# A four-layer hybrid trunk on one core: raw-x projections in the first mixer and paired score products in the attention

## The chip, the core and the metric

The kernel runs on one core of one Trainium2 chip, in one launch. Its metric is the device time in microseconds; less is better. An execution is a straight program: each engine works through its own list of instructions in order and waits on semaphores for the others. TensorE is called PE here, its weight loads PEld, VectorE is DVE, ScalarE is ACT, GpSimd is POOL, and SP issues most DMAs.

## What is computed

A trunk on x of 512 tokens by 1024 features, in float32: a gated DeltaNet mixer, a SwiGLU feed-forward, a dilated attention, and a second feed-forward. Each of the four normalises its input first and adds its output to x. The parts that the change touches:

```python
def _rmsnorm(x, w):
    y = x * lax.rsqrt(jnp.mean(x * x, axis=-1, keepdims=True) + RMS_EPS)
    return y * w
...
    proj = h @ w_in                      # h = _rmsnorm(x, w): q, k, v, gate z, and a, b
    qkv = jax.nn.silu(_causal_depthwise_conv(proj[..., :n_qkv], conv_w))
...
    o = o * norm_w * jax.nn.silu(z)      # o: the chunked delta rule, normalised
...
    scores = jnp.einsum("brnqhd,brnkhd->brnhqk", qb, kb) * (dh ** -0.5)
    logits = jnp.where(valid[:, None], scores + bias, -jnp.inf)
    p = jnp.exp(logits - m)              # m: the row maximum
```

The mixer has 8 heads of 128 features each for q, k, v and z. The attention has 24 heads of 64 features in three groups of 8: group 0 looks at the 128 last positions, groups 1 and 2 at every 4th and every 16th position further back. The factor of the norm, one number per token, can be taken out of a projection: (x * r) @ W = (x @ W) * r.

## The kernel before

Activations lie as features by tokens: a *page* is an SBUF tile of 128 features by 512 tokens, a *bank* one of PE's 8 accumulators of 128 by 512 float32. A projection is a *job* (`gemm_steps`, the matmul at L455): a weight tile, streamed in from HBM as `wraw`, is split into a high and a low half (`wh` by ACT, `wl` by DVE or POOL), the input likewise, and for each of 8 slices of the input three matmuls go into one bank: high·high, high·low, low·high. So a job is 24 matmuls of 512 columns.

The order of the work is set at build time by a planner, `Weave`. It runs generators against a simulated clock for each engine, and what they issue as they are resumed is the program's order. `W.run` runs a job on PE; between two of its matmuls all generators that have become ready get their turn, so other products stand between projection matmuls. `Banks` are counters that share the 8 banks out: `main` (`mm`) for jobs, `sm` for short products, `chain` (`ch`) for chains that hold one long. In the first mixer these are 2, 3 and 3 (`BANKS`), in the attention 3, 2 and 3 (`ABANKS`). The order of the jobs stands in `JOBS` (first mixer) and `DJOBS` (attention).

**First mixer** (`start` L302, `gdn` L505). When x has arrived, `highs` and `lows` (L393 and L404) make high and low halves of x times the norm's weight, the *raw* halves, which the first three key jobs use (`RAW_KEYS`). Meanwhile squares of x are summed and `rb`, the factor of the norm spread over 128 partitions, is worked out. Then `normalised` (L412) multiplies the eight pages of x by `rb`, five on POOL (`NORM`) and three on DVE, and `highs` and `lows` run a second time on these. The other 29 jobs use the second halves. A q, k or v job (`conv_job` L619) is followed by its `post`: ACT reads the bank with the last of four convolution taps, DVE adds the other three (for two key heads two, POOL the third), then comes SiLU through a tanh. The bank is given back only behind the last tap. In the three raw jobs DVE first multiplies the bank by `rb` into a page and gives it back at once:

```python
                    if raw:
                        yield "rb", 0
                        V.tensor_mul(dst, ps, self.rb)
                        main.release(V)
```

A finished key head is turned to tokens by PE (`turn`, L442) and multiplied with itself (`mat`, L437). `solve` (L734) inverts the triangular systems in 32-wide blocks on POOL and DVE, `merge` (L774) joins them on PE, and `head` (L872) runs the heads. The gate job (`gate_job` L978) reads its bank once on ACT (tanh) and once on DVE.

**Attention** (`dilated` L1085). Two heads share a page: head 0 in partitions 0 to 63, head 1 in 64 to 127; there are four such pairs for each group. `near(p, h)` (L1329) makes the scores of one head in group 0, in two bursts of products (`mat`, L437) into one bank each: blocks 0 and 1 (128 and 256 columns), then 2 and 3 (256 and 256). `far(p, h)` (L1375) makes those of groups 1 and 2, four products of 128 columns to a burst. Each burst is followed by DVE's addition of the distances and by row maxima, after which the bank is free. The weights of the distance (`near_rest`, `far_rest`), the values (`value` L1417) and the output (`project_job` L1478) follow. Three lanes (`DLANES`) of `near` and `far` run side by side: head 0's near, head 1's near, and far of both heads in turn. The output projection's first job holds three tiles and takes pairs 0 to 2 for all of them (27 matmuls) before pair 3.

Every DVE, ACT and POOL operation is recorded on one helper's line, L85 (L83 in the changed kernel, where L455, L442 and L437 become L441, L428 and L423).

Of the kernel before, what the change touches and what calls it, by code (L numbers as in the profile page):

```python
# [11 lines left out]
F32 = mybir.dt.float32  # L12
F32R = mybir.dt.float32r
I32 = mybir.dt.int32
AF = mybir.ActivationFunctionType
# [4 lines left out]
T = 512  # L20
# [3 lines left out]
H = 8  # L24
# [9 lines left out]
AHEAD = True  # L34
# [4 lines left out]
DLANES = ('n0', 'n1', 'f0 f1')  # L39
# [20 lines left out]
NORM = (1, 2, 4, 6, 7)  # L60
# [3 lines left out]
ABANKS = {'mm': 3, 'sm': 2, 'ch': 3}  # L64
# [110 lines left out]
class Trunk:  # L175
# [126 lines left out]
    def start(self):  # L302
# [90 lines left out]
        def highs(n):  # L393
            for k in range(KD):
                yield "ready", n, k
                if n == "raw":
                    yield max(RAW + PACE * k - W.now, 0.0)
# [28 lines left out]
        on_pool = NORM  # L426
        W.spawn(normalised(self.G, on_pool))
        W.spawn(normalised(self.V, [k for k in range(KD) if k not in on_pool]))  # L428
# [76 lines left out]
    def gdn(self):  # L505
# [4 lines left out]
        with tc.tile_pool(name="gk", bufs=1) as gk, tc.tile_pool(name="gw", bufs=2) as gw:  # L510
            self.start()
            events, raw_events = ([("x", n, k) for k in range(KD)] for n in (0, "raw"))
            tiles, raws = ([lambda n=n, k=k: self.xs[n, k] for k in range(KD)] for n in (0, "raw"))
# [105 lines left out]
            def conv_job(ft, dst, acc, then):  # L619

                yield main
                raw = ft < 2 * H and ft - H in RAW_KEYS
                if raw:
                    yield "weights", 0
                w = next(self.ws)
                ps = self.bank()
                yield from self.gemm_steps(ps, w, raws if raw else tiles, raw_events if raw else events)

                def post():
                    nonlocal ps  # L630
                    if raw:
# [19 lines left out]
                    if not raw:  # L651
                        main.release(0.0)
# [325 lines left out]
            def gate_job(h):  # L978
# [106 lines left out]
    def dilated(self):  # L1085
# [11 lines left out]
        with tc.tile_pool(name="ak", bufs=1) as ak, tc.tile_pool(name="aw", bufs=2) as aw:  # L1097
            dist, slopes, bones, wqk, eps, place, block = self.dc
            fac = lambda i: rr[:, i].rearrange("p (g c) -> p g c", g=3)[:, :, :, None].to_broadcast([128, 3, NCH, 2])
# [21 lines left out]
            pages, scores, spaces = Banks(W, APAGES), Banks(W, SCORES), Banks(W, VALUES)  # L1121
# [207 lines left out]
            def near(p, h):  # L1329

                f = slice(h * 64, (h + 1) * 64)
                yield "k", 0, p
                yield "rq", p
                ts = []
                mx = aw.tile([128, NCH], F32, name="mx0", bufs=8)
                for bs in ((0, 1), (2, 3)):
                    yield scores
                    yield sm
                    ps = self.bank()
                    t = aw.tile([128, T], F32, name="pp", bufs=SCORES)  # L1340
                    o = 0
                    spans = []
                    for b in bs:
                        k0 = max(b - 1, 0)
                        n = (b + 1 - k0) * 128
                        mat(ps[:, o:o + n], qT[0, p][f, ch(b)], kT[0, p][f, k0 * 128:(b + 1) * 128])
                        spans.append((b, o, n))
                        o += n
                    for b, o, n in spans:
                        V.scalar_tensor_tensor(t[:, o:o + n], dist[0][:, 256 - n:], sd[p][:, 0, b, h:h + 1],  # L1350
                                               ps[:, o:o + n], op0=OP.mult, op1=OP.add)
                        yield V.next()
                        V.reduce_max(mx[:, b:b + 1], t[:, o:o + n], axis=AX)
                        yield V.next()
                    sm.release(V)
                    ts.append((t, spans))
# [337 lines left out]
```

## Time and profile before

| | |
|---|---|
| median of 3 runs | 1410.41 us (1409.83 to 1410.54) |
| the profiled execution | 1408.56 us |
| its span | 1406.7 us |
| instructions | 18298 |
| busy: PE, PEld | 1370.3 us, 1128.7 us |
| busy: DVE, ACT, POOL | 810.4 us, 598.0 us, 275.3 us |

The profiled execution is one of its own, and its span is the time from the first to the last recorded instruction. The first mixer ends at about 350 us; the attention takes the stretch from about 715 to 1030 us, with most of its scores and values between 860 and 1011. Rows of the trace below name a line, an engine, an operation, the tiles written and read (`page<-bank,cp` reads a bank and a column of constants and writes a page) and their shapes.

### The profile page before, as it was taken

To read this page: it belongs to the slowest core of one execution; us is meant where nothing else is said; L and a number is where in the kernel's file an instruction comes from. 1 tells how busy PE (TensorE), PEld (TensorE's weight loads), DVE (VectorE), ACT (ScalarE), POOL (GpSimd) and SP (SyncE) were. 2 spreads that over 40 slices of the span, in tenths; PEclk is the share of its full clock that TensorE was granted. 3 is DMA by queue.
4 is the path that set the end of the run, shared out by engine and by line. 5 is a ranking of instruction groups with operands and counts; after the bars stand their busy time and mean duration, and the time that the engine had idled before them with its cause. 6 is when DMAs were issued, how large, how long until landed. Compare 5 with 4: busy or idle time off the path is not lost.

```text
span 1406.7 us, 18298 instructions
## 1 busy us (share of the span) xinstructions
PE 1370.3 (97%) x7040; PEld 1128.7 (80%) x7040; DVE 810.4 (58%) x1458; ACT 598.0 (43%) x1276; POOL 275.3 (20%) x239
## 2 busy tenths in 40 slices
PE   8799989999999999999999999999989999999998
PEld 5578878878888888888888878789968888888887
DVE  7987655767555455534446456887576554554222
ACT  4665465863333333322246445565533333332221
POOL 6543800124111111112112111100051111110000
PEclk9999999999999999999999999999999999999999
DMA  4124240134232323333332222111013323233331
GB/s 160 57 64 120 75 122 31 31 121 124 82 105 90 105 90 102 88 96 97 97 87 93 90 75 76 45 31 61 31 60 105 105 90 105 90 102 100 109 110 60
DMA packets 48328, 122.52 MB, mean 87 GB/s; under 512 B 16624, under 2 KB 17008, under 8 KB 48240
## 3 DMA queue, kind: packets, MB, share of 16 engines
q1 hardware_dynamic: 47952, 121.21, 28.3%
q8 instruction: 55, 0.90, 0.3%
q14 instruction: 33, 0.27, 0.1%
q10 hardware_dynamic: 288, 0.14, 0.0%
HBM read 117.66 MB, written 3.67 MB: 86 GB/s over the span
## 4 chain that ended last, share of the span: by engine, by line
PE 83%; DVE 8%; ACT 3%; POOL 3%; issue 2%; DMA 1%; SPq 0%; DVEq 0%; ACTq 0%; POOLq 0%
PE bank L455 69%; PE bank L437 8%; DVE page L85 5%; PE bank L1201 3%; PE bank L442 2%; POOL xblk L85 2%; POOL tblk L85 1%; ACT page L85 1%; DVE wl L85 1%; ACT wh L85 0%; DMA wraw<-in_w 0%; ACT pp L85 0%; DVE ro L85 0%; PE bank L1265 0%; DVE rsqrt L85 0%
## 5 line engine op out<-in xcount | busy, mean ns | idle before, releaser
L455 PE MATMUL bank<-page,wh 128*128 128x512 f32 x2912 | 947.5, 394 | 11.4 <-DVE page L85 8.5
L455 PEld LDWEIGHTS bank<-page,wh 128*128 128x128 f32 x2912 | 546.3, 189 | 128.6 <-DVE page L85 11.0
L455 PE MATMUL bank<-page,wl 128*128 128x512 f32 x1632 | 642.4, 394 | 3.4 <-DVE wl L85 2.9
L85 ACT ACTIVATE wh<-wraw 128x512 fp32r<-128x512 f32 (+1 forms) x432 | 255.8, 616 | 468.3 <-PE bank L455 263.7
L85 DVE TENSOR_TENSOR wl<-wraw,wh 128x512 fp32r<-128x512 f32 (+1 forms) x408 | 342.3, 859 | 165.6 <-ACT wh L85 165.2
L85 POOL TENSOR_TENSOR page<-page 128x512 f32<-128x512 f32 (+2 forms) x127 | 189.1, 1494 | 937.7 <-DVE page L85 556.4
L455 PEld LDWEIGHTS bank<-page,wl 128*128 128x128 f32 x1632 | 308.0, 189 | 69.3 <-DVE wl L85 5.8
L85 DVE TENSOR_TENSOR page<-bank,page 128x512 f32<-128x512 f32 (+1 forms) x115 | 79.2, 690 | 219.8 <-PE bank L455 212.5
L85 ACT ACTIVATE page<-page 128x512 f32<-128x512 f32 (+2 forms) x216 | 135.4, 630 | 122.1 <-POOL page L85 65.9
L455 PE MATMUL bank<-hl,wh 128*128 128x512 f32 x352 | 139.0, 395 | 0.0
L455 PEld LDWEIGHTS bank<-hl,wh 128*128 128x128 f32 x352 | 66.1, 188 | 14.0
L85 DVE TENSOR_TENSOR page<-page,bank 128x512 f32<-128x512 f32 x40 | 27.4, 686 | 73.3 <-PE bank L455 65.8
L85 DVE SCALAR_TENSOR_TENSOR page<-page,cp 128x512 fp32r<-128x512 f32 (+3 forms) x47 | 53.1, 1153 | 3.7 <-ACT page L85 3.7
L85 DVE SCALAR_TENSOR_TENSOR page<-bank,cp,page 128x511 f32<-128x511 f32 (+2 forms) x63 | 46.7, 742 | 8.6 <-ACT page L85 8.4
L437 PE MATMUL bank<-page 64*128 64x128 f32 (+2 forms) x320 | 50.7, 299 | 0.8 <-DVE page L85 0.8
L1201 PE MATMUL bank<-wh,page 128*128 128x256 f32 x256 | 48.3, 288 | 0.0
L85 ACT ACTIVATE pp<-pp,om,rq 128x128 f32<-128x128 f32 (+1 forms) x96 | 43.0, 509 | 11.4 <-DVE om L85 11.1
L437 PEld LDWEIGHTS bank<-page 64*128 64x128 f32 (+1 forms) x320 | 40.7, 189 | 8.8 <-issue 3.0
L85 ACT ACTIVATE page<-bank 128x512 f32<-128x512 f32 (+4 forms) x45 | 25.8, 573 | 51.4 <-PE bank L437 32.2
L85 DVE SCALAR_TENSOR_TENSOR pp<-dc,sd,bank 128x128 f32<-128x128 f32 (+1 forms) x96 | 33.8, 376 | 23.2 <-PE bank L437 22.7
L1201 PEld LDWEIGHTS bank<-wh,page 128*128 128x128 f32 x256 | 39.8, 191 | 1.8 <-issue 1.0
L85 POOL TENSOR_TENSOR wl<-wraw,wh 128x512 fp32r<-128x512 f32 x24 | 33.2, 1390 | 34.1 <-ACT wh L85 32.7
(174 smaller groups left out, 929.3 us busy)
## 6 DMA issues: line engine op xcount, KB each, us to landing
wraw<-in_fin SPq DMA_DIRECT2D x88, 512.0 KB, 3.6
wraw<-in_w SPq DMA_DIRECT2D x32, 512.0 KB, 3.6
wraw<-in_fout SPq DMA_DIRECT2D x32, 448.0 KB, 3.3
wraw<-in_dqk SPq DMA_DIRECT2D x24, 512.0 KB, 3.6
wraw<-in_fout SPq DMA_DIRECT2D x16, 512.0 KB, 3.6
wraw<-in_w0o SPq DMA_DIRECT2D x8, 512.0 KB, 3.6
wraw<-in_dv SPq DMA_DIRECT2D x8, 512.0 KB, 3.6
page<-in_x SPq DMA_DIRECT2D x8, 256.0 KB, 6.2
```

The lines of the kernel that those rows point to most:

```text
L85: return f(out, *args, **kw)
L437: self.nc.tensor.matmul(out, lhsT=lhsT, rhs=rhs, start=start, stop=stop)
L442: self.nc.tensor.transpose(out, in_, self.ident if ident is None else ident)
L455: self.nc.tensor.matmul(ps, lhsT=lhsT[:, c], rhs=rhs, start=k + i == 0, stop=k == len(xs) - 1 and i == 2)
L1201: self.nc.tensor.matmul(ps[c], lhsT=x[:, ch(c)], rhs=w[:, k * 256:(k + 1) * 256], start=b + k + t == 0, stop=b == 1 and k == 3 and t == 2)
```

## The change

In the first mixer all 32 projections take the raw halves; the second set of halves and the eight products x*rb are gone. Each bank is multiplied by `rb` on DVE afterwards instead: into a page with the bank given back at once for the first three key jobs, as before, and for the eight z gates; in place, in the bank, for the other 21 q, k and v jobs. In the attention `near` and `far` take both heads of a pair: their products are issued in turn, head 0 and head 1, into two banks, and the additions follow for one head and then the other. There are two lanes instead of three, a counter `both` that lets one pair take its two banks at a time, and `sm` has three banks and `ch` two. The planner's clock is set back after a pair (`W.now -=`), by what two products at once are taken to save.

```diff
-DLANES = ('n0', 'n1', 'f0 f1')
+DLANES = ('n', 'f')
...
-ABANKS = {'mm': 3, 'sm': 2, 'ch': 3}
+ABANKS = {'mm': 3, 'sm': 3, 'ch': 2}
...
-        def normalised(E, ks):
-            yield "rb", 0
-            for k in ks:
-                yield from self.room(E)
-                E.tensor_mul(self.x[k], self.x[k], self.rb)
-                W.fire(("ready", 0, k), E)
-
         W.spawn(gates())
-        for n in "raw", 0:
-            W.spawn(highs(n))
-            W.spawn(lows(n))
+        W.spawn(highs("raw"))
+        W.spawn(lows("raw"))
...
             def conv_job(ft, dst, acc, then):
...
-                yield from self.gemm_steps(ps, w, raws if raw else tiles, raw_events if raw else events)
+                yield from self.gemm_steps(ps, w, tiles, events)
 
                 def post():
                     nonlocal ps
-                    if raw:
-                        yield "rb", 0
+                    yield "rb", 0
+                    if early:
                         V.tensor_mul(dst, ps, self.rb)
                         main.release(V)
                         ps = dst
-                        yield V
+                    else:
+                        V.tensor_mul(ps, ps, self.rb)
+                    yield V
                     cw = lambda j: self.convw[:, ft * 4 + j:ft * 4 + j + 1]
                     S.activation(acc, ps, AF.Copy, scale=cw(3))
...
-                    if not raw:
+                    if not early:
                         main.release(0.0)
...
                     z, th = self.page(), self.page()
-                    S.activation(th, ps, AF.Tanh, scale=0.5)
+                    V.tensor_mul(z, ps, self.rb)
+                    main.release(V)
+                    yield V
+                    S.activation(th, z, AF.Tanh, scale=0.5)
                     yield S
-                    V.scalar_tensor_tensor(z, th, 1.0, ps, op0=OP.add, op1=OP.mult)
-                    main.release(V)
+                    V.scalar_tensor_tensor(z, th, 1.0, z, op0=OP.add, op1=OP.mult)
...
-            def far(p, h):
-
-                f = slice(h * 64, (h + 1) * 64)
+            def far(p):
+
                 yield "rq", p
...
                     yield scores
+                    yield scores
+                    yield both
                     yield sm
-                    ps = self.bank()
-                    t = aw.tile([128, T], F32, name="pp", bufs=SCORES)
+                    yield sm
+                    ps = [self.bank() for _ in range(2)]
                     for c in range(NCH):
-                        mat(ps[:, ch(c)], qT[g, p][f, ch(c)], kT[g, p][f, ch(c)])
-                    for c in range(NCH):
-                        V.scalar_tensor_tensor(t[:, ch(c)], dist[g], sd[p][:, g, c, h:h + 1], ps[:, ch(c)],
-                                               op0=OP.mult, op1=OP.add)
+                        for h in range(2):
+                            mat(ps[h][:, ch(c)], qT[g, p][half(h), ch(c)], kT[g, p][half(h), ch(c)])
+                    W.now -= 0.9 * 0.853
+                    both.release(0.0)
+                    for h in range(2):
+                        t = aw.tile([128, T], F32, name="pp", bufs=SCORES)
+                        for c in range(NCH):
+                            V.scalar_tensor_tensor(t[:, ch(c)], dist[g], sd[p][:, g, c, h:h + 1], ps[h][:, ch(c)],
+                                                   op0=OP.mult, op1=OP.add)
+                            yield V.next()
+                        sm.release(V)
+                        V.reduce_max(mx[h][:, g - 1], seg(t), axis=AX)
                         yield V.next()
-                    sm.release(V)
-                    V.reduce_max(mx[:, g - 1], seg(t), axis=AX)
```

`near` is changed in the same way as `far`. What the planner makes of it can be seen in the order of the instructions.

DVE in the first mixer, right behind the last step of the norm's factor, before. Here `page_313` is `rb`, `page_85` to `page_97` are pages of x, `bank_185` is the first key job's bank, `bank_329` that of the decay's inputs:

```order
L85 TENSOR_TENSOR page_85<-page_85,page_313 128x512
L85 TENSOR_TENSOR page_93<-page_93,page_313 128x512
L85 TENSOR_TENSOR page_97<-page_97,page_313 128x512
L85 TENSOR_TENSOR page_152<-bank_185,page_313 128x512
L85 TENSOR_TENSOR abt_334<-bank_329,nr_273 128x64
L85 SCALAR_TENSOR_TENSOR page_340<-page_85,cp_82,page_338 128x512
L85 SCALAR_TENSOR_TENSOR page_348<-page_87,cp_82,page_346 128x512
```

The same place now, with `bank_321` for the decay's inputs:

```order
L83 TENSOR_TENSOR page_152<-bank_185,page_313 128x512
L83 TENSOR_TENSOR abt_326<-bank_321,nr_273 128x64
L83 TENSOR_TENSOR y_127<-abt_326,cp_82 128x32
L83 SCALAR_TENSOR_TENSOR e_128<-y_127 128x32
L83 COPY e_128<-abt_326 128x32
L83 SCALAR_TENSOR_TENSOR page_153<-page_152,cp_82,page_153 128x511
```

The products on x and the low halves that stood behind them are gone: the first key bank is multiplied at once, and its first tap on DVE (`page_153`) follows four small instructions behind. Later on DVE, now, the first job that multiplies in place (k3, `bank_496`) meets the one whose bank comes free next (k7, `bank_415`):

```order
L83 COPY page_480<-bank_519 64x128
L83 MEMSET page_480 64x128
L83 SCALAR_TENSOR_TENSOR page_348<-page_348,page_349 128x512
L83 SCALAR_TENSOR_TENSOR page_411<-bank_415,cp_82,page_411 128x510
L83 TENSOR_TENSOR bank_496<-bank_496,page_313 128x512
L83 SCALAR_TENSOR_TENSOR page_411<-bank_415,cp_82,page_411 128x509
```

A product in place stands between the second and the third tap of k7, which still hold its bank.

PE in the attention, at a far burst before (`mat`, L437, the four products of one head into one bank), among projection matmuls and the sums of the key norms (L1165, L1166):

```order
L455 MATMUL bank_7420<-page_6147,wl_7378 128x512
L437 MATMUL bank_7462<-page_7370,page_6529 128x128 x4
L1165 MATMUL bank_7471<-page_7432,bones_3615 128x512
L1166 MATMUL bank_7471<-page_7433,bones_3615 128x512
L455 MATMUL bank_7485<-page_5431,wh_7425 128x512
```

The same burst now, with the products of the two heads into `bank_7452` and `bank_7453`:

```order
L441 MATMUL bank_7410<-page_6136,wl_7368 128x512
L423 MATMUL bank_7452<-page_7360,page_6518 128x128
L423 MATMUL bank_7453<-page_7360,page_6518 128x128
L423 MATMUL bank_7452<-page_7360,page_6518 128x128
L423 MATMUL bank_7453<-page_7360,page_6518 128x128
L423 MATMUL bank_7452<-page_7360,page_6518 128x128
```

The pair alternates between the heads, 8 products in all, and the other head's burst, which stood elsewhere before, is gone there.

PE at the end of the attention before, with the last value products (`pp` by `v`, L437) and the output projection's first matmuls (L455) between them:

```order
L442 MATMUL bank<-cc,pp 128x128 x8
L437 MATMUL bank<-pp,v_6120 128x128 x2
L455 MATMUL bank<-page,wh 128x512
L437 MATMUL bank<-pp,v_6120 128x128 x12
L437 MATMUL bank<-pp,v_6121 128x4x32
L437 MATMUL bank<-pp,v_6120 128x128 x2
L437 MATMUL bank<-pp,v_6121 128x4x32 x11
L455 MATMUL bank<-page,wh 128x512
L437 MATMUL bank<-pp,v_6121 128x4x32 x2
```

The same place now:

```order
L423 MATMUL bank<-pp,v_6110 128x4x32 x3
L441 MATMUL bank<-page,wh 128x512
L423 MATMUL bank<-pp,v_6110 128x4x32 x2
L441 MATMUL bank<-page,wl 128x512
L423 MATMUL bank<-pp,v_6110 128x4x32 x2
L441 MATMUL bank<-page,wh 128x512
L423 MATMUL bank<-pp,v_6110 128x4x32 x2
L441 MATMUL bank<-page,wh 128x512
```

Of the 27 matmuls on pairs 0 to 2, 2 stood ahead of the last value product before, and 16 do now.

## Rows read from the trace of the kernel before

**Rows 1.** the page's part 1: busy time (share of the span) and instructions of each engine.

```profile
PE 1370.3 (97%) x7040; PEld 1128.7 (80%) x7040; DVE 810.4 (58%) x1458; ACT 598.0 (43%) x1276; POOL 275.3 (20%) x239
```

**Rows 2.** busy time by stretch, columns as in the first line.

```profile
core 0: us, PE busy (x) PEld busy (x) DVE busy (x) ACT busy (x) POOL busy (x), PEclk, DMA share, GB/s
41.00:59.00 18.00, 10.10 (x42) 6.89 (x42) 18.00 (x25) 9.05 (x22) 9.74 (x6) 0.97 0.23 65
50.00:60.00 10.00, 6.54 (x29) 4.93 (x29) 10.00 (x15) 5.27 (x17) 5.52 (x4) 0.89 0.31 94
59.00:93.00 34.00, 32.46 (x156) 26.39 (x155) 29.45 (x67) 25.74 (x85) 15.94 (x17) 0.97 0.23 75
93.00:124.00 31.00, 31.00 (x172) 26.70 (x171) 22.72 (x61) 14.75 (x40) 8.24 (x8) 1.00 0.28 78
124.00:176.00 52.00, 52.00 (x244) 42.95 (x243) 34.09 (x46) 25.58 (x69) 41.70 (x66) 1.00 0.31 96
200.00:303.00 103.00, 99.89 (x790) 84.77 (x789) 72.51 (x232) 76.64 (x258) 10.08 (x7) 1.00 0.18 55
860.00:960.00 100.00, 99.63 (x577) 79.56 (x576) 79.92 (x226) 63.23 (x129) 9.64 (x7) 1.00 0.15 43
960.00:1011.00 51.00, 50.94 (x411) 48.43 (x410) 33.18 (x75) 28.02 (x59) 0.00 (x0) 1.00 0.17 53
```

**Rows 3.** PE's waits from 0 to 60 us: total, times, longest.

```profile
PE bank L455 <- DVE page L85: 5.0, 4, 2.4
...
PE bank L442 <- DVE page L85: 3.5, 2, 2.7
```

**Rows 4.** the chain that ended last: start, length, engine, line, instructions.

```profile
40.25 7.28 DVE page L85 x8
...
361.42 353.25 PE bank L455 x1552
```

**Rows 5.** DVE's groups by shape, 29 to 124 us: busy, mean ns, idle before.

```profile
L85 DVE SCALAR_TENSOR_TENSOR page<-page,cp 128x512 fp32r<-128x512 f32 x8 | 8.0, 1033 | 0.0
...
L85 DVE TENSOR_TENSOR page<-page 128x512 f32<-128x512 f32 x3 | 4.1, 1414 | 1.9 <-ACT page L85 1.9
...
L85 DVE TENSOR_TENSOR page<-bank,page 128x512 f32<-128x512 f32 x3 | 2.0, 677 | 0.0
```

**Rows 6.** timeline of PE, 58 to 64 us: start, length, instruction, wait.

```profile
58.26 1.08 PE L442 MATMUL bank<-cc,page 128*128 128x128 f32 x4 [2.73 <-DVE page L85]
...
61.25 0.62 PE L455 MATMUL bank<-page,wh 128*128 128x512 f32 x2
```

**Rows 7.** timeline of ACT, 106 to 107 us.

```profile
106.31 0.69 ACT L85 ACTIVATE page<-bank,cp 128x512 f32<-128x512 f32 x1 [0.23 <-PE bank L455]
```

**Rows 8.** timeline of DVE, 109 to 111 us.

```profile
110.09 0.74 DVE L85 SCALAR_TENSOR_TENSOR page<-bank,cp,page 128x509 f32<-128x509 f32 x1
```

**Rows 9.** timeline of PE, 178 to 180 us.

```profile
178.53 0.73 PE L455 MATMUL bank<-page,wh 128*128 128x512 f32 x2 [1.82 <-ACT wh L85]
```

**Rows 10.** timeline of PE in the attention, at three score bursts.

```profile
830.03 0.93 PE L437 MATMUL bank<-page 64*128 64x128 f32 x8 [0.58 <-DVE page L85]
830.90 0.50 PE L1201 MATMUL bank<-wh,page 128*128 128x256 f32 x2
...
882.27 0.92 PE L437 MATMUL bank<-page 64*128 64x128 f32 x4
883.12 0.55 PE L442 MATMUL bank<-cc,pp 128*128 128x128 f32 x3
...
885.45 1.16 PE L437 MATMUL bank<-page 64*128 64x128 f32 x8
886.53 0.66 PE L442 MATMUL bank<-cc,pp 128*128 128x128 f32 x4
```

**Rows 11.** timeline of PE at the attention's end, 1010 to 1018 us.

```profile
1010.81 0.48 PE L455 MATMUL bank<-page,wl 128*128 128x512 f32 x1
...
1017.37 0.50 PE L455 MATMUL bank<-page,wh 128*128 128x512 f32 x1 [0.60 <-ACT page L85]
```

More of the change, by code (lines that the diff above doesn't have):

```diff
@@ L395, in highs @@
                 yield "ready", n, k
-                if n == "raw":
-                    yield max(RAW + PACE * k - W.now, 0.0)
+                yield max(RAW + PACE * k - W.now, 0.0)
                 yield from self.room(self.S)
@@ L511, in gdn @@
             self.start()
-            events, raw_events = ([("x", n, k) for k in range(KD)] for n in (0, "raw"))
-            tiles, raws = ([lambda n=n, k=k: self.xs[n, k] for k in range(KD)] for n in (0, "raw"))
+            events = [("x", "raw", k) for k in range(KD)]
+            tiles = [lambda k=k: self.xs["raw", k] for k in range(KD)]
             ch = lambda c: slice(c * 128, (c + 1) * 128)
@@ L621, in conv_job @@
                 yield main
-                raw = ft < 2 * H and ft - H in RAW_KEYS
-                if raw:
+                early = ft < 2 * H and ft - H in RAW_KEYS
+                if early:
                     yield "weights", 0
@@ L1373, in near_rest @@
                 W.fire(("near", p, h), 0.0)
[L1375 to L1377 removed]
+            def far(p):
                 yield "rq", p
[L1379 to L1380 removed]
+                mx = [aw.tile([128, 2, NCH], F32, name="mx12", bufs=8) for _ in range(2)]
+                ts = [], []
                 for g in (1, 2):
@@ L1383, in far @@
                     yield scores
+                    yield scores
+                    yield both
                     yield sm
-                    ps = self.bank()
-                    t = aw.tile([128, T], F32, name="pp", bufs=SCORES)
+                    yield sm
+                    ps = [self.bank() for _ in range(2)]
                     for c in range(NCH):
-                        mat(ps[:, ch(c)], qT[g, p][f, ch(c)], kT[g, p][f, ch(c)])
-                    for c in range(NCH):
-                        V.scalar_tensor_tensor(t[:, ch(c)], dist[g], sd[p][:, g, c, h:h + 1], ps[:, ch(c)],
-                                               op0=OP.mult, op1=OP.add)
-                        yield V.next()
@@ L1393, in far @@
-                    sm.release(V)
-                    V.reduce_max(mx[:, g - 1], seg(t), axis=AX)
-                    yield V.next()
-                    ts.append(t)
-                if finished((p, "far"), 2):
-                    for _ in range(4):
-                        pages.release(0.0)
-                V.scalar_tensor_tensor(mx, mx, -1.0, rq[p][:, 1:, :, h], op0=OP.mult, op1=OP.mult)
-                yield V.next()
-                V.tensor_tensor(mx[:, 0], mx[:, 0], mx[:, 1], op=OP.min)
@@ L1403, in far @@
-                yield V.next()
-                W.spawn(far_rest(p, h, mx[:, 0], ts)) if AHEAD else (yield from far_rest(p, h, mx[:, 0], ts))
+                        for h in range(2):
+                            mat(ps[h][:, ch(c)], qT[g, p][half(h), ch(c)], kT[g, p][half(h), ch(c)])
+                    W.now -= 0.9 * 0.853
+                    both.release(0.0)
+                    for h in range(2):
+                        t = aw.tile([128, T], F32, name="pp", bufs=SCORES)
+                        for c in range(NCH):
+                            V.scalar_tensor_tensor(t[:, ch(c)], dist[g], sd[p][:, g, c, h:h + 1], ps[h][:, ch(c)],
+                                                   op0=OP.mult, op1=OP.add)
+                            yield V.next()
+                        sm.release(V)
+                        V.reduce_max(mx[h][:, g - 1], seg(t), axis=AX)
+                        yield V.next()
+                        ts[h].append(t)
@@ L1498, in lane @@
                     for s in steps.split():
-                        yield from {"n": near, "f": far}[s[0]](p, int(s[1]))
+                        yield from {"n": near, "f": far}[s](p)
             self.nc.scalar.preload_act_table_set("natural_log_exp_and_others")
```

54 lines of the change are left out of this document (27 added, 27 removed).

## The prediction, made before the changed kernel was run

> **What bounds the kernel now.** The profile's first part comes first: TensorE (PE) is busy 97% of the span, far ahead of VectorE (DVE), ScalarE (ACT) and GpSimd (POOL) [rows 1]. So time can come from three places only: PE's own work made shorter, the 3% in which it stands still, and the stretches at its lower clock. The busy time by stretch says where the change can reach them [rows 2]. From 41 to 59 us PE is busy 10.10 of 18.00 us while DVE is busy all 18.00; from 860 to 1011, the attention, PE is full (99.63 of 100 and 50.94 of 51) and DVE is at 79.9% and then 65%. PE's waits in the first 60 us name what the first hole is: 5.0 us of projection matmuls (L455) and 3.5 us of the turns of finished heads (L442) wait for DVE [rows 3]. The chain that ended last agrees: from 40.25 on it runs for 7.28 us through eight DVE instructions [rows 4], which have the length of the eight low halves of the normalised x, 8.0 us by shape [rows 5].
>
> **First mixer, what goes.** Before, 29 of 32 projections need the normalised x, so DVE does three x*rb products (4.1 us) and eight low halves (8.0 us) right where the first heads' convolutions also need it [rows 5]; the turns wait because their convolutions stand behind these in DVE's order. Raw halves exist already for the first three key jobs. With them the 5.0 us and the 3.5 us have no cause left: **−8.5**. Nothing else is then late at once, since the raw halves are finished before rb. After the hole PE also ran at its low clock: the granted clock is 0.89 from 50 to 60 [rows 2], and the four turn matmuls at 58.26 take 1.08 us. Projections run at full rate again from 61.25 [rows 6]. Those 2.99 us at the lower of its two levels would take half: **−1.5**. The removed work of ACT (8 high halves) and POOL (5 products) I price at nothing: from 41 to 59 they are busy 9.05 and 9.74 of 18.00 us [rows 2], so DVE's queue hides them; without that cover their eight steps would set the low halves' pace, and with the change both are gone together.
>
> **First mixer, what comes.** A product of a bank and rb takes 0.677 us on DVE [rows 5]; there are 29 new ones: 21 in place, in the bank, and 8 for the z gates, whose bank is free after the product, as it was after the one gate instruction before. Until 124 us DVE loses 12.1 us and gains some ten of these (6.8), so its total falls. The new cost is in the banks. A job is 24 matmuls at 353.25/1552 = 0.2276 us [rows 4], 5.46 us, and two banks take turns. The first reading of a bank (ACT, 106.31, 0.23 after PE's end) [rows 7] and the last convolution tap on DVE (ends 110.83) [rows 8] show one held for 4.75 us after its job. Plus 0.68 and about 0.2 of hand-over that is 5.6, against 5.46 in which the other bank's job runs. So the cover is just used up, and PE feels each DVE backlog longer than that. In the changed order the product for k3's bank stands between two taps that still hold k7's, which I price at two products: **+1.5**. Its ends are 0, if the taps come early, and 1.2 us on each of 21 jobs, if not (a rival below).
> Two smaller costs. From the last key product to the first 32-wide merge, PE's order has 269 projection matmuls instead of 274, 1.1 us less cover for POOL's triangular solve (41.70 of 52 us busy from 124 to 176, [rows 2]); PE waits 1.82 us at its end already [rows 9]: half of it, **+0.5**, between 0 and 1.1. In the heads' stretch, 200 to 303, seven more products add 4.8 us to a DVE busy 72.51 of 103, where PE already stands 3.1 us [rows 2]: a quarter of it, **+1.2**, between 0 and 4.8. First mixer: −8.5 − 1.5 + 1.5 + 0.5 + 1.2 = **−6.8**.
>
> **Paired products.** A score product uses 64 of 128 partitions. The trace has one place where the near products of both heads (128 and 256 columns each) come one behind the other, from 830.03 to 830.90: 0.87 us for two heads. One head alone takes from 882.27 to 883.12, 0.85. So heads on different halves run together. A burst of 512 columns of one head takes 885.45 to 886.53, 1.08 [rows 10]. Before: 16 far bursts and 8 second near ones at 1.08, 8 first near ones at 0.85, less the 0.83 of the one pair that overlaps: 31.9. After: 8 + 4 pairs at 1.08 and 4 at 0.87: 16.4. PE's work falls by **15.5**.
> Two things take from it. The tail: the output projection's first 27 matmuls (pairs 0 to 2 of three tiles) fill PE while the last head's output is made ready. Now 25 of them come after the last value product, at 1010.81, and the next one needs pair 3 and starts at 1017.37 after a wait of 0.60 [rows 11]. In the new order 11 are left there, so the same chain shows 14 × 0.2276 = **+3.2**, a wait of 3.8; 0 if that chain gets as much shorter, no more than 5.7 (all 25).
> The second is DVE, which must empty the score banks at the old pace: 79.92 + 33.18 = 113.1 us of work over 151 [rows 2], 75%, and over 151 − 15.5 = 135.5 it is 83%. At 79.9% PE stood 0.37 of 100 us; at 87% (59 to 93) it stood 1.54 of 34, which over 135.5 would be 6.1. Nearer the first row: **+2.0**, with 0.4 and 6.1 as ends. The Trainium skill (TensorEngine Tiling (Array Packing), PSUM Bottleneck) speaks against the change here: tiling speeds TensorE but not the emptying of PSUM, which may become the limit. By that rule as a bound at today's DVE share the time would be that of the first rival; the rows of now, PE full beside a DVE at 79.9%, don't yet bear it out. Attention: −15.5 + 3.2 + 2.0 = **−10.3**.
> The smaller changes (two lanes for three, ABANKS, the planner's credits) carry no instruction of their own and only set the order.
>
> **Sum.** −6.8 − 10.3 = −17.1 on the profiled 1408.56 us: 1391.5. The median of the runs stands 1.85 above the profiled one, so 1391.5 + 1.85 = **1393.3 us**. A measurement of this kernel tells 0.2%, 2.8 us, from no change.
>
> **Rivals.**
> *DVE bounds the attention.* If it can't get past a share of 77%, a little over the mean of now, its 113.1 us take 146.9, 4.1 less than 151, and the tail takes 3.2 back. For it: the work on the score banks is unchanged and two banks now fill at once. Against: 87% was reached from 59 to 93. −6.8 − 0.9: **1402.7**.
> *The first mixer gives nothing.* Bank holds and heads return all that the hole gave: −10.3 alone, **1400.1**. For: the held 5.6 against 5.46. Against: DVE has 12.1 us less to do early.
> *Both are given back:* −0.9, **1409.5**, no change.
> *Slower: two banks too few.* Place: the `mm` banks of the first mixer. Each of the 21 in-place jobs keeps its bank one product longer, and DVE works in order, so a tap may stand behind another job's product (0.68) and its hand-over and a tap of 0.74. At 1.2 us of PE per job this costs 25.2 in place of 1.5: −8.5 − 1.5 + 0.5 + 1.2 + 25.2 − 10.3 = +6.6, **1417.0**. The other terms gain 18.6, so it decides from 18.6/21 = 0.89 us per job on. For: DVE at 29.45 of 34 from 59 to 93. Against: 22.72 of 31 after it and 34.09 of 52 after that [rows 2], room enough for most of these jobs.
>
> **How the numbers follow.** The forecast has a chance of 0.60: each of its gains has a wait or a pair of bursts in the trace behind it. DVE as bound 0.16, first mixer nothing 0.12, both given back 0.04, slower 0.08. Faster by over 0.2%: 0.60 + 0.16 + 0.12 = 0.88; same 0.04; slower 0.08. Low end: all gains, no cost, 1410.41 − 8.5 − 1.5 − 15.5 = 1384.9, less the 1.54 us for which PE stands from 59 to 93: 1383. High end: past the 1402.7 of the first rival, 1404. Outside lie the last two cases and little of the others.
>
> **What would show it.** Right: no wait of L455's counterpart for DVE from 41 to 59, and the matmul that now waits 1.82 us for a weight tile at 178.53 [rows 9] some 7 us earlier; score bursts of eight products on two heads in 1.1 us; the attention stretch 13 us shorter with DVE above 80%; before the first output matmul of pair 3 a wait of 3 to 4 us. Wrong: PE waits for a bank after each projection job between 60 and 180 (the last rival); PE waits for DVE at the score bursts, with DVE still near 77% (the first); paired bursts that take 2 us, that is, run one after the other.

## The result and the profile after

The changed kernel takes 1394.4 us (median of 4 runs, 1390.27 to 1394.93), the kernel before 1410.12 beside it: 0.9882 of it, with a 95% interval of 0.9863 to 0.9902. It is faster by some 16.6 us; the forecast was 1393.3. Two more series of it on other chips (changed_again and changed_third below) gave 0.9884 and 0.9878. But the two parts did not give what was forecast for each.

PE's work has become shorter, against [rows 1] by 12.3 us, and DVE's has stayed:

```profile
PE 1358.0 (98%) x7040; PEld 1121.7 (81%) x7040; DVE 811.9 (58%) x1476; ACT 591.9 (43%) x1268; POOL 265.8 (19%) x234
```

The chain that ended last tells the parts apart, since both feed-forwards begin with a long unbroken piece of matmuls in it. In the kernel before (the first piece is in [rows 4], at 361.42; here the key heads' hand-over to the solve through memory, and the second feed-forward):

```profile
127.82 3.47 DMA mblk<-scr
...
1053.71 349.38 PE bank L455 x1536
```

and in the changed kernel (start, length, what):

```profile
122.80 3.59 DMA mblk<-scr
...
357.91 353.25 PE bank L441 x1552
...
1039.27 349.38 PE bank L441 x1536
```

The key heads are done 5.0 us earlier, the first feed-forward starts 3.5 us earlier (361.42 to 357.91), the second 14.4. So the first mixer gave 3.5 us where 6.8 were forecast, and the attention 14.4 − 3.5 = 10.9 where 10.3 were. The stretches that answer to [rows 2], with its columns, and one more at 35 us:

```profile
35.00:40.00 5.00, 3.14 (x16) 2.33 (x15) 4.90 (x9) 1.26 (x3) 3.07 (x2) 1.00 0.11 24
41.00:59.00 18.00, 17.64 (x78) 13.97 (x78) 15.23 (x34) 11.63 (x39) 11.71 (x13) 0.92 0.21 64
59.00:93.00 34.00, 31.52 (x162) 25.59 (x161) 28.91 (x59) 21.87 (x69) 13.77 (x11) 1.00 0.25 77
...
124.00:176.00 52.00, 50.93 (x233) 41.00 (x232) 38.23 (x50) 28.22 (x75) 40.00 (x62) 1.00 0.35 111
...
860.00:960.00 100.00, 98.98 (x699) 83.58 (x696) 88.81 (x249) 68.38 (x140) 8.17 (x6) 1.00 0.18 50
960.00:1011.00 51.00, 47.99 (x320) 41.88 (x319) 29.86 (x62) 26.53 (x53) 5.63 (x5) 0.93 0.15 49
```

From 41 to 59 PE is now busy 17.64 of 18 us where it was 10.10: the hole is gone. In the attention PE still has no idle time to speak of, 1.02 of 100 us, beside a DVE at 88.8%.

**What remains of the first hole.** The 5.0 us of projections behind DVE of [rows 3] are gone from PE's waits in the first 60 us. The turns' waits are not; PE's waits in that stretch, total, times and longest:

```profile
PE bank L428 <- DVE page L83: 2.2, 2, 1.9
```

With 2.2 us more before 130 us they make 4.4. In the kernel before it was 3.5 up to 60 us [rows 3] and 1.4 from there to 130. The first is in PE's timeline:

```profile
39.62 0.66 PE L428 MATMUL bank<-cc,page 128*128 128x128 f32 x4 [1.86 <-DVE page L83]
...
41.22 1.05 PE L441 MATMUL bank<-page,wh 128*128 128x512 f32 x2
...
44.45 0.62 PE L441 MATMUL bank<-page,wh 128*128 128x512 f32 x2
```

The first key head is turned at 39.62. In the kernel before it was turned at 51.43, since its convolution and the low halves were mixed in DVE's order. DVE's groups by shape from 40 to 47.5 us, before, show the mixture:

```profile
L85 DVE SCALAR_TENSOR_TENSOR page<-page,cp 128x512 fp32r<-128x512 f32 x4 | 3.8, 988 | 0.0
L85 DVE SCALAR_TENSOR_TENSOR page<-page,cp 128x510 f32<-128x510 f32 x1 | 1.8, 1777 | 0.0
```

So the piece of 7.28 us in [rows 4] is not the eight low halves for which the prediction took it. It is four of them, the three taps of the first key head (the one above and two of 0.74 us) and one product of a bank and `rb` (0.68). Of these only the low halves go with the change. Now PE comes so early that DVE, busy 4.90 of 5 us from 35 to 40, is still at that head's convolution and at the decay's small steps.

Behind this wait of 1.86 us PE works at its lower clock until about 44 us: a pair of 512-column matmuls shows 1.05 us there and 0.62 behind it. So in this execution the low clock has come earlier and not gone. It is not so in every one: in changed_third, whose first turn waits 1.87 us as well, the granted clock from 41 to 59 is 1.00, and so it is in changed_again and raw_alone:

```profile
41.00:59.00 18.00, 16.48 (x77) 12.61 (x75) 15.64 (x33) 12.49 (x40) 12.55 (x14) 1.00 0.20 60
```

From the first turn to the key heads' hand-over it takes 83.2 us with the low clock (39.62 to 122.80) and 82.4 without (39.26 to 121.64 in changed_third; the same in the other two): it costs 0.8 us there. At 179.89 there is a second wait of this kind, where before one of 1.33 us stood at 184.50, again with a stretch at low clock behind it:

```profile
179.89 0.79 PE L428 MATMUL bank<-cc,page 128*128 128x128 f32 x4 [2.48 <-DVE page L83]
```

**The pairs.** Timeline of PE at a near and a far pair, each with the instruction behind it:

```profile
884.16 1.14 PE L423 MATMUL bank<-page 64*128 64x256 f32 x8
885.22 0.98 PE L428 MATMUL bank<-cc,pp 128*128 128x128 f32 x7
...
893.23 1.16 PE L423 MATMUL bank<-page 64*128 64x128 f32 x16
894.32 0.71 PE L423 MATMUL bank<-pp,v 128*128 128x128 f32 x4
```

Sixteen records, two heads' far products, take 1.09 us, as one head did in [rows 10]; the near pair takes 1.06. Over the whole attention the score bursts take 16.4 us in 16 pieces, and 31.5 in 30 before: 15.1 less, where 15.5 were forecast.

**The tail.** PE behind the last value product, to be read with [rows 11]:

```profile
994.73 0.48 PE L441 MATMUL bank<-page,wh 128*128 128x512 f32 x1
...
999.86 1.52 PE L441 MATMUL bank<-page,wh 128*128 128x512 f32 x2 [2.34 <-ACT page L83]
...
1001.60 1.05 PE L441 MATMUL bank<-page,wh 128*128 128x512 f32 x2
...
1007.23 0.62 PE L441 MATMUL bank<-page,wh 128*128 128x512 f32 x2
```

The wait is 2.34 us, where it was 0.60. From the first matmul behind the last value product (994.73) to pair 3 there are 5.13 us, where there were 6.56 (1010.81 to 1017.37 in [rows 11]), so the last pair's chain has become 1.4 us shorter. What was not forecast stands behind it: until about 1006.5 the matmuls run at half speed. The busy times of these 10 us have a granted clock of 0.66 (last column but two):

```profile
998.00:1008.00 10.00, 8.14 (x22) 6.16 (x23) 5.91 (x8) 3.85 (x7) 3.50 (x3) 0.66 0.00 0
```

### The profile page after: what moved, and what is told of

Same layout as the page of the kernel before. It is cut to its first block, busy times and chain, and to the rows that moved or that the text cites. A ratio compares the mean times of both kernels' runs of the same rounds, so it can differ in the third digit from the quotient of the medians.

```text
span 1392.3 us, 18305 instructions
## 1 busy us (share of the span) xinstructions
PE 1358.0 (98%) x7040; PEld 1121.7 (81%) x7040; DVE 811.9 (58%) x1476; ACT 591.9 (43%) x1268; POOL 265.8 (19%) x234
## 4 chain that ended last, share of the span: by engine, by line
PE 84%; DVE 7%; ACT 3%; POOL 3%; issue 2%; DMA 1%; SPq 0%; DVEq 0%; ACTq 0%; POOLq 0%
PE bank L441 71%; PE bank L423 7%; DVE page L83 4%; PE bank L1192 3%; PE bank L428 2%; POOL xblk L83 2%; POOL tblk L83 1%; ACT page L83 1%; DVE wl L83 1%; ACT pp L83 1%; DMA wraw<-in_w 0%; ACT wh L83 0%; PE bank L1256 0%; DVE rsqrt L83 0%; DVE pp L83 0%
## 5 line engine op out<-in xcount | busy, mean ns | idle before, releaser
L83 POOL TENSOR_TENSOR page<-page 128x512 f32<-128x512 f32 (+2 forms) x122 | 179.0, 1470 | 923.0 <-DVE page L83 559.4
L83 DVE TENSOR_TENSOR page<-bank,page 128x512 f32<-128x512 f32 (+1 forms) x123 | 84.7, 690 | 228.8 <-PE bank L441 216.9
L83 ACT ACTIVATE page<-page 128x512 f32<-128x512 f32 (+2 forms) x224 | 140.4, 629 | 123.1 <-POOL page L83 65.9
L83 DVE SCALAR_TENSOR_TENSOR page<-page,cp 128x512 fp32r<-128x512 f32 (+3 forms) x39 | 45.0, 1166 | 3.7 <-ACT page L83 3.7
L83 DVE SCALAR_TENSOR_TENSOR page<-page 128x512 f32<-128x512 f32 (+1 forms) x52 | 41.8, 804 | 1.1 <-ACT page L83 0.3
L83 ACT ACTIVATE page<-bank 128x512 f32<-128x512 f32 (+4 forms) x37 | 21.0, 568 | 42.1 <-PE bank L423 28.7
L1192 PE MATMUL bank<-wl,page 128*128 128x256 f32 x128 | 36.4, 284 | 1.0 <-DVE wl L83 0.9
```

Source lines behind the costliest of these rows:

```text
L83: return f(out, *args, **kw)
L1192: self.nc.tensor.matmul(ps[c], lhsT=x[:, ch(c)], rhs=w[:, k * 256:(k + 1) * 256], start=b + k + t == 0, stop=b == 1 and k == 3 and t == 2)
```

## The experiments

All are compared with the kernel before, on the same chip at the same time. A difference of 0.003 in the ratios is within the noise of most.

| run | median, us | ratio | 95% interval |
|---|---|---|---|
| changed kernel | 1394.40 | 0.9882 | 0.9863 to 0.9902 |
| raw_alone | 1405.38 | 0.9973 | 0.9963 to 0.9982 |
| pairs_alone | 1398.09 | 0.9916 | 0.9901 to 0.9931 |
| in_turn | 1397.78 | 0.9917 | 0.9905 to 0.9929 |
| tail_fill | 1391.78 | 0.9875 | 0.9859 to 0.9891 |
| changed_again | 1391.83 | 0.9884 | 0.9868 to 0.9899 |
| tail_four | 1393.45 | 0.9895 | 0.9880 to 0.9909 |
| fill_waits | 1392.48 | 0.9892 | 0.9876 to 0.9907 |
| tail_four_fill | 1397.15 | 0.9923 | 0.9906 to 0.9940 |
| changed_third | 1392.49 | 0.9878 | 0.9863 to 0.9893 |
| two_products | 1393.60 | 0.9892 | 0.9877 to 0.9907 |
| page_all | 1397.43 | 0.9916 | 0.9902 to 0.9931 |
| fill_two | 1390.56 | 0.9865 | 0.9849 to 0.9882 |

The theory behind them: the raw halves take away PE's waits for the second halves and no more, because DVE's own work on the key heads is next; two heads' products overlap when they stand together; and waits of PE are paid twice where its clock falls behind them. The rivals: held banks, DVE as the bound in the attention, and a gain that belongs to both parts together.

### One part alone

raw_alone is the changed kernel with the attention of the kernel before, pairs_alone the other way round. A cut of raw_alone's edit, against the changed kernel:

```diff
-DLANES = ('n', 'f')
-ABANKS = {'mm': 3, 'sm': 3, 'ch': 2}
+DLANES = ('n0', 'n1', 'f0 f1')
+ABANKS = {'mm': 3, 'sm': 2, 'ch': 3}
...
+            def near(p, h):
+            def far(p, h):
```

Expected of raw_alone:

> Only the first mixer is changed; the attention is that of the kernel before. If the two parts add up as the trace of the changed kernel has it (the first feed-forward begins 3.5 us earlier there), 1410.1 - 3.5 = 1406.6 us, and no low clock before the second output projection. Rival, the forecast's own term: 6.8 less, 1403.3 us. Rival, the gain belongs to both parts together: within 1 us of 1410.1.

Expected of pairs_alone:

> Only the attention is changed; the first mixer is that of the kernel before. Theory: the score products give what they gave in the changed kernel, with the wait of about 2.3 us behind the last value product and about 6 us of low clock after it: 1410.1 - 11 = 1399.1 us. If the clock stays up there, 3.2 us less, 1396 us. Rival, the attention gains only behind an earlier first mixer: over 1402 us.

Measured: 0.9973 is 3.8 us less (2.5 to 5.2), 0.9916 is 11.8 less (9.7 to 14.0). The product of the ratios is 0.9889, the whole change's 0.9882: the parts add up, and neither needs the other. The forecast's 6.8 for the first mixer lies outside its interval, its 10.3 for the attention inside. PE's wait for the turns in the first 130 us of raw_alone, total, times and longest:

```profile
PE bank L429 <- DVE page L84: 4.5, 4, 1.9
```

With 4.5 us it is that of the changed kernel (2.2 + 2.2), and in the kernel before it was 3.5 + 1.4. In this execution the clock is full at 40 us, and still the first feed-forward begins at 358.03, 3.4 us earlier than before: the first mixer gave no more in it, though no low clock stands behind the first turn.

### Head by head into the same banks

in_turn issues all products of head 0 and then all of head 1. The cut shows `far`; `near` is changed in the same way.

```diff
-                    for c in range(NCH):
-                        for h in range(2):
+                    for h in range(2):
+                        for c in range(NCH):
                             mat(ps[h][:, ch(c)], qT[g, p][half(h), ch(c)], kT[g, p][half(h), ch(c)])
```

> The changed kernel, but each pair issues all products of head 0 and then all of head 1, into the same two banks. Theory, that it is enough that the two heads stand next to each other (the one such place of the kernel before took 0.87 us for two heads in this order): the time of the changed kernel within 1 us, bursts of 1.1 us. Rival, that they must alternate: the two heads run one after the other, bursts of 2.2 us, 15 us more, about 1410 us.

PE's timeline at a near and a far pair of it:

```profile
886.72 1.14 PE L423 MATMUL bank<-page 64*128 64x256 f32 x8
...
895.79 1.71 PE L423 MATMUL bank<-page 64*128 64x128 f32 x16
897.42 0.71 PE L423 MATMUL bank<-pp,v 128*128 128x128 f32 x4
```

Neither theory holds. A near pair, two products of 256 columns per head, still takes 1.1 us: there it is enough that the heads stand together. A far pair, four of 128 columns per head, takes 1.63 to the next instruction, between the 1.09 of alternating heads and the 2.16 of two heads apart. Eight far pairs at 0.54 more are 4.3 us; by the ratios the run is 0.9917 − 0.9882 = 0.0035, 5 us, above the changed kernel. So part of the gain is the neighbourhood, and for long bursts the alternation is worth those 4 to 5 us.

### The bank that is held

two_products does each product in place twice; page_all writes it into a page and gives the bank back.

```diff
                     else:
+                        V.engine.tensor_mul(dst, ps, self.rb)
                         V.tensor_mul(ps, ps, self.rb)
```
```diff
-                    if early:
-                        V.tensor_mul(dst, ps, self.rb)
-                        main.release(V)
-                        ps = dst
-                    else:
-                        V.tensor_mul(ps, ps, self.rb)
+                    V.tensor_mul(dst, ps, self.rb)
+                    main.release(V)
+                    ps = dst
```

Expected of the changed kernel beside them, of two_products and of page_all:

> The changed kernel beside the next three on the same chip: 0.988 of the kernel before, as twice already.

> The changed kernel with the product of bank and rb done twice in each of the 21 in-place jobs (the first result, in a page, is overwritten unread): 0.68 us more of DVE per job, in which the bank is held too; 14.3 us of DVE in all. Theory: nothing waits for these banks, and DVE is on the path only up to the last key head, some 7 jobs: 2 to 5 us slower than the changed kernel. Rival, each job's bank is waited for: 14 us slower. Rival, all of it is covered: within 1 us.

> The changed kernel with the 21 products written into a page, as in the three early jobs, so that the bank is given back at once and DVE's taps read the page (0.74 to 1.45 us in the trace of before, where a tap from a bank takes 0.74). If the held banks cost the 1.5 us of the forecast: 1 to 1.5 us faster than the changed kernel. Theory, that banks cost nothing and DVE is the path up to the last key head: 2 to 6 us slower.

Twice the product costs 0.0014, 2 us (by the far ends of the two intervals 6 at most), of the 14.3 us of DVE work that it adds: the rival of 0.9 us and more per job is out. The forecast's own term for held banks finds no wait either: none of PE's projections waits for DVE up to 130 us, and up to 360 only two do, for pages of the output projection (0.99 us at 300.44, 0.22 at 308.11). page_all is 0.0038, 5 us, slower, and its interval lies clear of that of the changed kernel beside it. Its busy times while POOL solves the triangular systems, and those of two_products:

```profile
124.00:176.00 52.00, 48.37 (x225) 38.90 (x223) 42.84 (x48) 23.67 (x67) 44.40 (x60) 1.00 0.29 91
```
```profile
124.00:176.00 52.00, 50.18 (x232) 40.27 (x231) 43.26 (x59) 27.78 (x70) 40.39 (x63) 1.00 0.33 102
```

The loss is not where it was expected: the key heads are done at 123.33, the first feed-forward begins only at 363.79. A fuller DVE does not explain it, since in two_products DVE is as full (43.26 of 52) and PE stands for 1.82 us there and not for 3.63. What differs is POOL. The chain that ended last has, from the hand-over to the first instruction behind the solve, in page_all:

```profile
123.33 3.51 DMA mblk<-scr
...
176.74 2.01 ACT mblk L83
```

and in the changed kernel (its hand-over is at 122.80, above):

```profile
171.35 2.11 ACT mblk L83
```

These are 53.4 us in place of 48.6, and the solve's 62 POOL instructions take 44.9 us in place of 40.0 (40.3 in two_products). So taps that read pages go along with a slower solve on POOL, and these 4.9 us are the 5 that page_all loses. Banks given back early gained nothing that could be seen beside it.

### Work put into PE's waits

tail_fill puts 11 matmuls that nobody reads ahead of the output projection's pair 3, fill_waits puts some into four waits, fill_two into two of them. The cut is that of tail_fill:

```diff
                         yield from self.gemm_steps(p, w2[f], tiles, events, k0=k0, k1=k1, base=f % 2 * -4)
+                    if len(fs) == 3 and k0 == 0:
+                        yield sm
+                        spare = self.bank()
+                        for i in range(FILL):
+                            self.nc.tensor.matmul(spare, lhsT=w2[0][0][:, :128], rhs=os_[0][0], start=i == 0, stop=i == FILL - 1)
```

> The changed kernel with 11 more matmuls of 512 columns, whose result nobody reads, between the output projection's matmuls on pairs 0 to 2 and those on pair 3: 2.5 us of work in a wait of 2.34 us. Theory: the low clock from 999.9 to 1006 follows from the wait, so it goes, 3.2 us less and 0.2 us more for the work: about 1391.4 us. Rival, the clock falls there anyway: 1394.6 us. Rival, the matmuls only stand in the way: 1396.9 us.

PE's timeline of tail_fill at that place:

```profile
999.15 2.65 PE L1500 MATMUL bank<-page,wh 128*128 128x512 f32 x11
...
1002.39 0.50 PE L442 MATMUL bank<-page,wh 128*128 128x512 f32 x1 [0.23 <-DVE page L84]
...
1002.96 0.62 PE L442 MATMUL bank<-page,wh 128*128 128x512 f32 x2
```

The 11 matmuls (L1500) fill the wait to within the 0.23 that pair 3's low half takes, and behind them a pair of matmuls shows 0.62, the full clock. At its place the theory holds. In the total it can't be seen: 0.9875, and 0.9882, 0.9884 and 0.9878 for the changed kernel without them.

> The changed kernel once more, beside the next three on the same chip: 1394.4 us, 15.7 less than before. Its runs should differ by what they lose at the low clock: stretches of it at the start, near 40, 180, 1000 and 1030 us.

> The changed kernel with matmuls that nobody reads put into four waits of PE in its own order: 8 before the first key head's turn (a wait of 1.86 us at 39.6), 11 before the turn at 179.9 (2.48 us), 11 before the output projection's pair 3 (2.34 us), 15 before the second feed-forward's last input (3.37 us). Theory: low clock follows on such waits and costs 1.7, 1.7, 3.4 and 3.4 us there, which all come back: 10 us less than the changed kernel, 1384.4 us. Rival, the clock falls elsewhere or as often: the time of the changed kernel within 1 us. Rival, the turns are late by the matmuls in front of them: up to 1.5 us more.

Here too the clock stays up behind all four waits, and the profiled execution is at 1391.77 us nevertheless. Two things were given back. The 15 matmuls of the second feed-forward stood behind the wait and not in it:

```profile
1024.81 0.50 PE L452 MATMUL bank<-page,wh 128*128 128x512 f32 x1 [3.37 <-DVE page L86]
...
1031.09 3.58 PE L290 MATMUL bank<-page 128*128 128x512 f32 x15
```

and at the first turn the clock's gain ends in a wait for the decay's factors on DVE (`g`), while the turn itself comes 0.6 us later than in the changed kernel:

```profile
38.19 1.98 PE L290 MATMUL bank<-page 128*128 128x512 f32 x8
40.23 0.65 PE L439 MATMUL bank<-cc,page 128*128 128x128 f32 x4
...
46.54 0.38 PE L434 MATMUL bank<-g,cc 128*128 128x32 f32 x2 [0.59 <-DVE g L86]
```

So the low clock behind the first turn cost little: DVE is the path there. The same wait for `g`, 0.6 us, stands in changed_again, changed_third and raw_alone, where the clock is full at 40 us without any filling. fill_two keeps the tail's matmuls and puts those of the feed-forward where PE waits:

> The changed kernel with matmuls that nobody reads in two waits of PE only: 10 before the output projection's pair 3 and 14 before the second feed-forward's matmuls on x's slice 6, where PE really waits (the 15 of the earlier run stood behind that wait and cost 3.4 us). Theory: the low clock behind these two waits, 1.7 to 3.4 us at each, comes back, and the matmuls fit into the waits: 3 to 6 us faster than the changed kernel. Rival, the clock then falls elsewhere: within 1 us of it.

PE's longest wait from 975 to 1045 us of it:

```profile
PE bank L455 <- DVE wl L86: 1.0, 1, 1.0
```

The two waits of 2.3 and 3.4 us are filled and the clock holds there, but in this execution it fell at 20, 40, 176 and 986 us. With 0.9865 it has the lowest ratio of all, 1.9 us under the changed kernel on its chip, and their intervals overlap: not shown to be faster.

### Useful work in the last wait

tail_four lets the output projection's first job hold four tiles, tail_four_fill adds matmuls that nobody reads in the other three waits.

```diff
-LAST = ((0, 1, 2), (3,), (4,), (5,), (6,), (7,))
-LBANKS = {'mm': 3, 'sm': 2, 'ch': 3}
+LAST = ((0, 1, 2, 3), (4,), (5,), (6,), (7,))
+LBANKS = {'mm': 4, 'sm': 2, 'ch': 2}
```

> The changed kernel with four output tiles in the output projection's first job in place of three (4 mm banks, 2 sm, 2 ch there): 9 more useful matmuls, 2.05 us, behind the last value product. Theory: the wait of 2.34 us there shrinks to about 0.3 and the low clock behind it (3.4 us) goes: 5.4 us less than the changed kernel, 1389 us. Rival, only the wait shrinks: 1392.3 us. Rival, the two chains that are left hold up the last pair: 1394 us or more.

> The four tiles of the run before last with the matmuls before the two turns and before the second feed-forward's last input, without those before pair 3. If both work and add up: 5.4 + 1.7 + 1.7 + 3.4 = 12.2 us less than the changed kernel, 1382.2 us. Rival, that only the useful matmuls help: 1389 us.

Both miss; tail_four's time is near that of its last rival, but the place is another. PE's waits of tail_four from 975 to 1045 us:

```profile
PE bank L441 <- ACT page L83: 3.7, 2, 1.9
PE bank L441 <- DVE wl L83: 3.6, 1, 3.6
PE bank L441 <- DVE page L83: 2.6, 3, 1.4
```

and of the changed kernel:

```profile
PE bank L441 <- DVE page L83: 3.4, 1, 3.4
PE bank L441 <- ACT page L83: 2.6, 2, 2.3
PE bank L441 <- DVE wl L83: 0.4, 1, 0.4
```

9.9 us in place of 6.4: the longest wait for ACT is still 1.9 us, and a weight tile and x are late behind it, on DVE, which now has four tiles to add and to split at once. The work was moved from one wait to the next. tail_four_fill is slower still, 5 us above the changed kernel. Its trace shows what can be most of that: the 15 matmuls for the second feed-forward start at 1033.51 and take 3.6 us, behind a wait of 3.03 us at 1028.14 and not in it. No run shows it by itself.

### How the low clock differs from one execution to the next

The three profiled executions of the changed kernel, cut into stretches of 2 us, lose at low clock (the sum of 2 us times one minus the granted clock, where this is under 0.97) 13.6, 10.3 and 5.1 us up to 1380 us; the kernel before 6.8. Their spans are 1392.3, 1391.2 and 1388.0. The first and the third differ at the tail's wait; PE's timeline of the third (changed_third), to be held against the tail above:

```profile
998.70 0.50 PE L441 MATMUL bank<-page,wh 128*128 128x512 f32 x1 [2.32 <-ACT page L83]
...
999.99 0.63 PE L441 MATMUL bank<-page,wh 128*128 128x512 f32 x2
```

2.32 us of waiting, then full speed. The chain that ended last of this execution:

```profile
356.78 353.26 PE bank L441 x1552
...
1034.99 349.38 PE bank L441 x1536
```

Here the first mixer gave 361.42 − 356.78 = 4.6 us and the attention 1053.71 − 1034.99 − 4.6 = 14.1. The 3.2 us between this and the 10.9 above have two places. From pair 3 to the next long wait of PE, 3.4 us in both, the first execution takes 28.0 us (999.86 to 1027.90) and the third 26.0 (998.70 to 1024.68): 2.1 us for the low clock at the tail. The other 1.1 come behind that wait, where both run at low clock, the first for longer (3.4 us lost by the sum above, and 1.7).

## Why the prediction was right, and where it was not

- **The total** was within 1.1 us, and in part by luck: errors of both signs met. The first mixer gave 3.8 us alone, where 6.8 were forecast, and the attention 11.8, where 10.3 were.
- **The hole at 41 us: −8.5.** This step failed. "With them the 5.0 us and the 3.5 us have no cause left" is true of the 5.0 alone. Nearly half of the 7.28 us piece that was read as low halves is the first key head's own convolution. The turns wait for the key heads' convolutions, which are DVE's own work; without the halves ahead of them PE comes earlier and waits again, 4.4 us in all after 4.9. The key heads are done 5.0 us earlier (6.2 in changed_third), not 8.5, and the matmul that waited for a weight tile at 178.53 starts at 175.02, 3.5 us earlier and not 7.
- **The low clock behind it: −1.5.** About half of it was gained at best. The stretch behind 58 us went; in the profiled execution one at 40 us came, behind the same kind of wait. Where none came the key heads were done 0.8 us earlier by it, and a part went into the wait for the decay's factors on DVE.
- **Held banks: +1.5.** Nothing was lost: no wait of PE's projections for DVE up to 130 us, and 2 us, within the noise, for twice the product. The rival on the slower side falls with it.
- **Solve and heads: +1.7.** From the key heads' end to the first feed-forward 1.5 us were lost (5.0 to 3.5). The size is right and the working only in part: a wait of 2.48 us at 179.89 (1.33 before) and 1.7 us at low clock behind it lie in this stretch, which I had not in the sum.
- **The pairs: −15.5.** It was 15.1, as worked out from one place in the trace where two heads stood together.
- **The tail: +3.2.** It was 1.7: the wait grew from 0.60 to 2.34, not to 3.8, since the last pair's chain got 1.4 us shorter, which the prediction had named as what could bring the term down.
- **DVE in the attention: +2.0.** In the 100 us from 860 PE stands 0.65 us more than before, which over the 135.5 us of the prediction would be 0.9, an estimate. DVE reached 88.8%, so the rival with a share of 77% is out. The rule of the Trainium skill (TensorEngine Tiling (Array Packing), PSUM Bottleneck) that emptying PSUM may become the limit, which it states for a fourfold speed-up, does not show here with two products at once: PE was busy 98.98 of those 100 us.
- **What was missing:** the clock behind the tail's wait. Up to the end of that wait all executions agree: from the first feed-forward's start to pair 3 it took 655.95 us before (361.42 to 1017.37) and 641.92 to 641.95 in the three executions of the changed kernel, 14.0 less. From pair 3 to the second feed-forward it took 36.34 us before and 39.41, 37.31 and 36.29 in the three, so the low clock gives back up to 3.1 us. The terms as measured, −15.1, +1.7 and about +0.9 for DVE, make −12.5 of the 14.0. What the other 1.5 us are stays open. The 14 fewer changes between score and projection matmuls could be part of it, and the lanes and bank counters were changed alone in no run.

## What to carry to other kernels

A wait that disappears is worth only the time until the next thing that the same instruction needs: ask for each waiting instruction what its producer still has to do once the named cause is gone. Products that use half of the partitions should be issued alternately for the two halves, and be close together in any case. Filling an idle stretch kept the clock up here, but no run shows that it made the kernel faster; it gives nothing where what stands behind the stretch waits for the same late producer. And look at more than one execution before a stretch at low clock is taken for a property of the kernel.

## What the runs showed of the hardware

- Matmuls on partitions 0 to 63 and 64 to 127 overlap even when they are not alternated: two products per head in a block lose nothing (1.1 us), four lose half of the gain (1.63 between 1.09 and 2.16).
- The same wait was followed by half speed in one execution of the same kernel and by full speed in another: 2.3 us at the tail, and 1.9 us at 40 us. In the three executions of the changed kernel each stretch of low clock lost 1.7 or 3.4 us by the sum above, and less of it reached the path: 0.8 of the 1.7 at 40 us, 2.1 of the 3.4 at the tail. The rest is covered where PE waits for DVE a little later anyway.
- The same 62 POOL instructions took 44.9 us beside DVE taps that read pages, and 40.0 to 40.3 beside taps that read banks, with DVE equally full (42.84 and 43.26 of 52 us) in page_all and two_products.
